# The first weights of each way up loaded on another queue, and three tiles in turn for one FFN factor

## The chip, the cores and the metric

One Trainium2 chip, one core. The metric is the device time of one execution in microseconds (us), as the median of timed runs. The engines are PE (matrix engine), VectorE (DVE), ScalarE (ACT), GpSimd (POOL) and SyncE (SP, which here only issues transfers). Each takes its own instructions strictly in order; they meet at semaphores. ScalarE, GpSimd and SyncE can issue transfers.

## The reference

Two transformer blocks over one sequence of 1024 rows of width 1024, in float32. What the change touches are the feed-forward parts; the mixers are left out here.

```python
def first_block(x, c, w_ada, ...):
    ...                                     # norm, three mixers, w_out, residual
    h = rms_norm(x, g_pre_ffn[l]) * (1.0 + sc_f) + sh_f
    up = dwconv3(h @ w_up[l], conv_w[l], conv_b[l])   # w_up: 1024 x 5632
    gate, val = jnp.split(up, 2, axis=-1)
    y = (jax.nn.gelu(gate) * val) @ w_down[l]         # 2816 x 1024
    x = x + gt_f * rms_norm(y, g_post_ffn[l])

def dwconv3(h, w, b):   # over positions, width 3, zero padded
    hp = jnp.pad(h, ((0, 0), (1, 1), (0, 0)))
    return hp[:, :-2] * w[0] + hp[:, 1:-1] * w[1] + hp[:, 2:] * w[2] + b

def _swiglu(x, w1, w3, w2):
    return (jax.nn.silu(x @ w1) * (x @ w3)) @ w2      # 1024 -> 2816 -> 1024

def second_block(x, ...):
    x = _layernorm(DEEPNORM_ALPHA * x + 0.5 * _swiglu(x, ffn1_w1[l], ffn1_w3[l], ffn1_w2[l]), ...)
    ...                                     # sparse attention and gated MLP, w_out
    x = _layernorm(DEEPNORM_ALPHA * x + 0.5 * _swiglu(x, ffn2_w1[l], ffn2_w3[l], ffn2_w2[l]), ...)
```

## The kernel before

The kernel goes through five large stages: the first block's mixer, the first block's FFN (`ffn1`), the second block's first FFN (`swiglu`), its mixer, and its second FFN (`swiglu` again). In the text T1 is the stretch in which `ffn1` begins, T2 that in which the first `swiglu` begins, T3 that in which the second one begins.

Every FFN has a way up and a way down. The way up is `up()`. It makes 22 output tiles f (128 hidden columns of each of the two factors, over 1024 positions), each out of seven products P = 1 to 7 of Strassen's scheme in Winograd's form, in the order 1, 2, 6, 7, 4, 5, 3. One product is 12 matmuls of 128 x 512: four slices of depth, each in three terms (`mm3`, lines 111 to 113), since every float32 operand is split into a high and a low half. Of the weights, ScalarE makes the high half `wh` (line 87) and VectorE or POOL the low half `wl` (line 106); POOL does it for products 1 and 5. POOL also makes the sums `T` of weight blocks that the products 4, 6, 7 need (line 264). Of the activations, `cross_xt()` transposes the normalised rows on PE (line 223) and makes the sums and halves `s23h`, `s23l`, `s4h`, `s4l` with POOL (lines 228, 231, 237), VectorE and ScalarE.

The weights of two tiles f come in one load of 1 MB for each factor: `load_cols` (line 125), 128 x 8 x 256 into a buffer `raw`. All of these loads are issued by POOL: with an engine given, `load_cols` pins the load into POOL's program order (`keep_in_program_order`), behind everything that the program wrote ahead of it for POOL. The first two loads of a way up (f = 0) are written at the start of `up()`, after the work of the stage before. In T1 the work ahead of them on POOL is the loop of `right()`, which prepares sums of the down weights in DRAM (`td`; lines 423, 432, 434). In T2 it is the additions of line 1724, which belong to the way down of `ffn1`.

Behind each f the products are added together (line 92, mostly VectorE) into the tiles 0 and 1 of `acc`, a buffer of eight tiles of 128 x 1024. In `ffn1` the function `glue` then makes both factors: `conv` is one ScalarE activation (line 1670) and two VectorE steps (line 101), g goes through gelu on ScalarE (line 1683), v is convolved likewise, and g becomes g·v (line 92, 128 x 1024). g lies in tile 2 and v in tile 3 of `acc` for even f, in 4 and 5 for odd f. `left()` then takes the two g tiles of a pair of f, makes their Winograd sums and stores them to `gd` in DRAM (`put`, line 389, on SP). The g tile of the even f is called e there: it takes up two of the sums (e + g and g − e), and the store of these is the last thing that reads it.

The order of instructions on each engine comes from a scheduler that goes by priorities and readiness, except for what is pinned. SP's own loads and stores are not pinned.

Of the kernel before, what the change touches and what calls it, by code (L numbers as in the profile page):

```python
# [20 lines left out]
FF = 2816  # L21
# [17 lines left out]
class Kern:  # L39
# [544 lines left out]
    def swiglu(self, w1, w3, w2, h1, ln, last, base, init, scale=None, bias=None, spill=None, during=None):  # L584


        tc, nc, acc = self.tc, self.nc, self.acc
        gd = self.dram.tile([NF // 2, 128, 7, 512], F32, name="gd" + ln[0])
        td = self.dram.tile([NF // 2, 128, 2, 1024], F32, name="td" + ln[0])

        def glue(f, P=None, done=None, c=None):
            g, v = acc[:, f % 2, :], acc[:, 2, :]
            if P is None:
                return g, v, g
            if P in (2, 4):
                nc.scalar.activation(out=g[:, c], in_=g[:, c], func=AF.Silu)
            if P != 2 and done >= ({2, 3} if P == 3 else {4, 5}):
                self.tt(g[:, c], g[:, c], v[:, c], OP.mult)

        self.stemps = self.unit_rows((3, 4))[:3]  # L600
        with tc.tile_pool(name="up", bufs=1, reuse_waits="tile") as pool:
            self.up(pool, [lambda f, w=w: self.load_cols(w, f * 128, eng=nc.gpsimd) for w in (w1, w3)], h1, glue,
                    scale, bias, gd, during, below=(w2, td))
        with tc.tile_pool(name="dn", bufs=1, reuse_waits="tile") as pool:
            for t in range(8):
                nc.gpsimd.dma_start(out=acc[:, t, :], in_=base[t * 128:(t + 1) * 128, :])
            tail = self.ln_tail(pool, ln, 4.0 * LN_EPS, last)
            self.down(pool, gd, td, w2, h1, tail, init, lambda: self.t4(pool, 5))
            if spill is not None:
                for t in range(8):  # L610
                    nc.gpsimd.dma_start(out=spill[t * 128:(t + 1) * 128, :], in_=acc[:, t, :])
# [1038 lines left out]
    def ffn1(self):  # L1650
        tc, nc, A = self.tc, self.nc, self.A
        xh, xl, acc = self.xh, self.xl, self.acc
        wu = A["w_up"][0]
        gd = self.dram.tile([NF // 2, 128, 7, 512], F32, name="gd")
        self.x2r = self.dram.tile([S, D], F32, name="x2r")
        self.stemps = self.unit_rows((6, 7))
        with tc.tile_pool(name="up", bufs=1, reuse_waits="tile") as pool:
            rows = [self.part(i, [88, 128]) for i in range(2)]
            for i in range(4):
                src = A["conv_w"][0, i] if i < 3 else A["conv_b"][0]  # L1660
                nc.scalar.dma_start(out=rows[i // 2][(i % 2) * 44:(i % 2) * 44 + 44, :],
                                    in_=src.rearrange("(r p) -> r p", p=128))
            ps = self.bankB([128, 2, 88])
            for i in range(2):
                nc.tensor.transpose(ps[:, i, :], rows[i], self.ident[:88, :88])
            cw = []

            def conv(u, h, j):

                nc.scalar.activation(out=u, in_=h, func=AF.Identity, scale=cw[0][:, 44 + j:45 + j],  # L1670
                                     bias=cw[0][:, 132 + j:133 + j])
                self.stt(u[:, 1:], h[:, :-1], cw[0][:, j:j + 1], u[:, 1:], OP.mult, OP.add)
                self.stt(u[:, :-1], h[:, 1:], cw[0][:, 88 + j:89 + j], u[:, :-1], OP.mult, OP.add)

            def glue(f, P=None, done=None, c=None):
                o = 2 + f % 2 * 2
                g, v = acc[:, o, :], acc[:, o + 1, :]
                h = [acc[:, i, :] for i in range(2)]
                if P is None:
                    return *h, g  # L1680
                if P in (2, 4) and done >= {2, 4}:
                    conv(g, h[0], f)
                    nc.scalar.activation(out=g, in_=g, func=AF.Gelu_apprx_tanh)
                elif P == 3:
                    conv(v, h[1], NF + f)
                    self.tt(g, g, v, OP.mult)

            def start():
                cw.append(pool.tile([128, 176], F32, name="cw"))
                self.copy(cw[0], ps.rearrange("p a b -> p (a b)"))  # L1690

            self.up(pool, [lambda f, o=o: self.load_cols(wu, o + f * 128, eng=nc.gpsimd) for o in (0, FF)], 0, glue,
                    self.gs_f, self.sh_f, gd, start=start)
        with tc.tile_pool(name="dn", bufs=1, reuse_waits="tile") as pool:
            pair = []
            gt = pool.tile([128, 1024], F32, name="gt")
            nc.sync.dma_start(out=gt, in_=self.gf_row.to_broadcast([128, 1024]))

            def room4():
                return pool.tile([128, 1024], F32, name="uv", tag="uv", bufs=4)  # L1700

            def tail(n, t):
                x = self.t4(pool, 2)
                nc.sync.dma_start(out=x, in_=self.x1d[t * 128:(t + 1) * 128, :])
                pair.append((t, x))
                if n == 0:
                    self.ss, self.junk = pool.tile([128, 8], F32, name="rss"), room4()
                with tc.high_priority() if n > 5 else nullcontext():
                    normed(n, t)
                if n % 2 and n < 4:  # L1710
                    self.later.append((n + LAG, lambda: self.keep_xt(t // 2)))

            def normed(n, t):
                a = acc[:, t, :]
                self.sumsq(self.ss[:, n:n + 1], a, self.junk)
                if n % 2 == 0:
                    return
                ss = self.ss[:, n - 1:n + 1]
                self.ts(ss, ss, 1.0 / D, OP.mult, RMS_EPS, OP.add)
                r = self.rsqrt(pool, ss, 2, "r2")  # L1720
                for i, (u, x) in enumerate(pair[-2:]):
                    a = acc[:, u, :]
                    self.stt(a, a, r[:, i:i + 1], gt, OP.mult, OP.mult)
                    (nc.vector if n > 5 else nc.gpsimd).tensor_tensor(out=a, in0=a, in1=x, op=OP.add)
                    nc.sync.dma_start(out=self.x2r[u * 128:(u + 1) * 128, :], in_=a)

            self.down(pool, gd, self.td, A["w_down"][0], 0, tail, None, room4)
# [737 lines left out]
```

## Time and profile before

| what | value |
|---|---|
| timed runs, median of 3 | 3225.34 us (3224.27 to 3226.1) |
| profiled execution, its own time | 3220.59 us |
| span of its trace | 3218.8 us |
| busy share: PE, VectorE, ScalarE, POOL | 91%, 74%, 39%, 36% |

The page of the profile gives busy times over the whole span. The rows further down are from narrower views: a table of busy times by stretch, timelines of one engine (each row is an instruction or a run of like ones, with the idle time before it and what ended that in brackets), and the table of waits (engine, line and tile that waited, what it waited for, the total, how often, the longest). "<-DMA x<-y" means that a transfer from y to x was waited for.

### The profile page before, as it was taken

What the parts mean: (1) busy time and instruction counts of PE and PEld (TensorE: products, weight loads), DVE (VectorE), ACT (ScalarE), POOL (GpSimd) and SP (SyncE); (2) the same over time, 40 slices, a digit from 0 to 9 for tenths busy, and PEclk for the clock granted to TensorE, in tenths of its full rate; (3) what the DMA queues carried; (4) which work ended last, traced back from release to release, by engine and by line L of the source; (5) the groups of instructions that cost most, each with busy time, mean ns of one, the idle gap of its engine ahead of it and who ended that gap; (6) DMA issues with size and microseconds to landing.
All of it is one profiled execution on the core that took longest, in us unless ns stands there. A gap on an engine that the chain in (4) does not pass through costs nothing. (4 is left out here: it accounts for less than half of the span.)

```text
span 3218.8 us, 38064 instructions
## 1 busy us (share of the span) xinstructions
PE 2932.0 (91%) x13810; PEld 2317.2 (72%) x13810; DVE 2368.8 (74%) x3855; ACT 1249.0 (39%) x2023; POOL 1168.6 (36%) x1001
## 2 busy tenths in 40 slices
PE   6899996799898999699999999977999799999996
PEld 4675565677777887578887888875677677887885
DVE  6982656887878656877776577799857887777567
ACT  5122532433333443323222443557762422222442
POOL 4422267655544002645553001131313655453003
PEclk9899998899999999799999999989999899999998
DMA  6116364222222673344444773110012265444762
GB/s 212 55 34 246 136 199 156 72 87 84 93 85 91 233 229 133 118 161 151 152 159 168 253 246 105 41 34 1 14 68 104 78 237 190 156 160 167 264 213 88
DMA packets 175508, 440.18 MB, mean 137 GB/s; under 512 B 16296, under 2 KB 36040, under 8 KB 175192
## 3 DMA queue, kind: packets, MB, share of 16 engines
q1 hardware_dynamic: 138924, 307.20, 27.4%
q0 software_dynamic: 36032, 130.19, 12.3%
q8 instruction: 109, 1.79, 0.2%
q14 instruction: 79, 0.65, 0.1%
q10 hardware_dynamic: 364, 0.35, 0.0%
HBM read 315.41 MB, written 122.27 MB: 136 GB/s over the span
## 5 line engine op out<-in xcount | busy, mean ns | idle before, releaser
L87 ACT ACTIVATE wh<-raw 128x512 fp32r<-128x512 f32 (+1 forms) x506 | 407.3, 826 | 839.6 <-PE bB L112 207.9
L106 DVE TENSOR_TENSOR wl<-raw,wh 128x1024 fp32r<-128x1024 f32 (+1 forms) x370 | 439.3, 1193 | 245.0 <-ACT wh L87 243.6
L111 PE MATMUL bB<-xh,wh 128*128 128x512 f32 (+1 forms) x860 | 343.3, 399 | 4.7 <-ACT xh L87 4.5
L112 PE MATMUL bB<-xl,wh 128*128 128x512 f32 (+1 forms) x860 | 340.3, 396 | 4.2 <-DVE xl L106 4.2
L113 PE MATMUL bB<-xh,wl 128*128 128x512 f32 (+1 forms) x860 | 339.5, 395 | 0.7 <-DVE wl L106 0.6
L92 DVE TENSOR_TENSOR acc<-acc 128x512 f32<-128x512 f32 (+2 forms) x306 | 306.7, 1015 | 19.6 <-DMA gdln_g<-acc 9.5
L106 POOL TENSOR_TENSOR wl<-raw,wh 128x512 fp32r<-128x512 f32 (+1 forms) x136 | 220.7, 1625 | 220.1 <-ACT wh L87 210.3
L111 PE MATMUL bA<-xh,wh 128*128 128x512 f32 (+1 forms) x508 | 211.4, 417 | 90.0 <-DVE acc L92 53.3
L264 POOL TENSOR_TENSOR T<-raw 128x512 f32<-128x512 f32 x132 | 200.1, 1516 | 182.9 <-DMA raw<-in_ffn_w 96.4
L92 DVE TENSOR_TENSOR acc<-bA,acc 128x512 f32<-128x512 f32 x226 | 150.4, 685 | 127.4 <-PE bA L113 127.1
L92 DVE TENSOR_TENSOR acc<-bB,acc 128x512 f32<-128x512 f32 x260 | 178.1, 686 | 69.2 <-PE bB L113 58.7
L264 POOL TENSOR_TENSOR T<-raw,T 128x512 f32<-128x512 f32 x66 | 106.8, 1619 | 309.4 <-DVE wl L106 307.0
L112 PE MATMUL bA<-xl,wh 128*128 128x512 f32 (+1 forms) x508 | 208.2, 411 | 1.0 <-DVE xl L106 1.0
L113 PE MATMUL bA<-xh,wl 128*128 128x512 f32 (+1 forms) x508 | 207.8, 409 | 0.2 <-DVE wl L106 0.2
L111 PEld LDWEIGHTS bB<-xh,wh 128*128 128x128 f32 x860 | 164.0, 191 | 46.8 <-ACT xh L87 6.0
L112 PEld LDWEIGHTS bB<-xl,wh 128*128 128x128 f32 x860 | 163.6, 190 | 44.6 <-DVE xl L106 5.9
L87 ACT ACTIVATE wh<-T 128x512 fp32r<-128x512 f32 x198 | 118.2, 624 | 191.9 <-PE bA L112 88.9
L113 PEld LDWEIGHTS bB<-xh,wl 128*128 128x128 f32 x860 | 163.4, 190 | 39.5 <-DVE wl L106 1.3
L111 PEld LDWEIGHTS bA<-xh,wh 128*128 128x128 f32 x508 | 101.5, 200 | 122.6 <-ACT wh L87 73.2
L101 DVE SCALAR_TENSOR_TENSOR acc<-acc,cw 128x1023 f32<-128x1023 f32 x88 | 138.6, 1576 | 62.2 <-ACT acc L1670 61.7
L111 PE MATMUL bA<-wh 128*128 128x512 f32 x432 | 170.5, 395 | 12.8 <-DVE acc L92 12.8
L112 PE MATMUL bA<-wl,wh 128*128 128x512 f32 x432 | 169.7, 393 | 0.0
(527 smaller groups left out, 7401.9 us busy)
## 6 DMA issues: line engine op xcount, KB each, us to landing
raw<-in_ffn_w POOLq DMA_DIRECT2D x44, 1024.0 KB, 6.1
raw<-gdln_g SPq DMA_DIRECT2D x70, 512.0 KB, 4.1
raw<-in_w_up POOLq DMA_DIRECT2D x22, 1024.0 KB, 6.2
tq<-in_ffn_w SPq DMA_DIRECT2D x44, 512.0 KB, 4.9
tdln_g<-tq SPq DMA_DIRECT2D x44, 512.0 KB, 2.6
gdln_g<-acc SPq DMA_DIRECT2D x44, 512.0 KB, 2.6
raw<-tdln_g SPq DMA_DIRECT2D x40, 512.0 KB, 5.0
raw<-gd SPq DMA_DIRECT2D x35, 512.0 KB, 4.0
```

The lines of the kernel that those rows point to most:

```text
L87: self.nc.scalar.activation(out=out, in_=in_, func=AF.Copy)
L92: self.nc.vector.tensor_tensor(out=out, in0=a, in1=b, op=op)
L101: self.nc.vector.scalar_tensor_tensor(out=out, in0=a, scalar=s, in1=b, op0=op0, op1=op1)
L106: (eng or self.nc.vector).tensor_tensor(out=lo, in0=src, in1=hi.bitcast(F32), op=OP.subtract)
L111: mm(out, lhsT=wh, rhs=xh, start=start, stop=False)
L112: mm(out, lhsT=wh, rhs=xl, start=False, stop=False)
L113: mm(out, lhsT=wl, rhs=xh, start=False, stop=stop)
L264: sub = lambda o, a, b: nc.gpsimd.tensor_tensor(out=o, in0=a, in1=b, op=OP.subtract)
```

## The change

Two edits. First, in both ways up the two loads of f = 0 are issued without an engine given, so they go to SP's queue and aren't pinned; the loads of all later f stay on POOL. Second, in `ffn1` the tile of g is 2, 3 or 4 by f modulo 3, and v always has tile 5.

```diff
@@ swiglu
-            self.up(pool, [lambda f, w=w: self.load_cols(w, f * 128, eng=nc.gpsimd) for w in (w1, w3)], h1, glue,
+            self.up(pool, [lambda f, w=w: self.load_cols(w, f * 128, eng=f and nc.gpsimd) for w in (w1, w3)], h1, glue,
                     scale, bias, gd, during, below=(w2, td))
@@ ffn1, glue
-                o = 2 + f % 2 * 2
-                g, v = acc[:, o, :], acc[:, o + 1, :]
+                g, v = acc[:, 2 + f % 3, :], acc[:, 5, :]
                 h = [acc[:, i, :] for i in range(2)]
@@ ffn1
-            self.up(pool, [lambda f, o=o: self.load_cols(wu, o + f * 128, eng=nc.gpsimd) for o in (0, FF)], 0, glue,
+            self.up(pool, [lambda f, o=o: self.load_cols(wu, o + f * 128, eng=f and nc.gpsimd) for o in (0, FF)], 0, glue,
                     self.gs_f, self.sh_f, gd, start=start)
```

How this moves instructions, at three places. SP's queue between the last loads of the first mixer (`in_w_out`) and the stores of its result rows (`x1d`), as the difference:

```order
 L1596 DMA raw<-in_w_out 128x1024 x3
 L1600 DMA raw<-in_w_out 64x1024 x4
+L125 DMA raw<-in_w_up 128x8x256 x2
 L1642 DMA x1d<-t_3070 128x1024
 L1642 DMA x1d<-t_3157 128x1024
```

The two first loads of the first FFN now stand ahead of all the stores of the mixer's result. POOL at the same transition, where `tq` and `td` belong to the loop of `right()`:

```order
 L432 TENSOR_TENSOR tq<-tq 128x256 x4
 L434 DMA td<-tq 128x2x256 x2
-L125 DMA raw<-in_w_up 128x8x256 x2
 L106 TENSOR_TENSOR wl<-raw,wh 128x512 x2
 L228 TENSOR_TENSOR raw<-acc 128x256 x2
```

POOL's rows around them keep their order; only the loads are gone. POOL in T2, with the additions of the way down (`acc` plus a residual row tile `t_...`), before:

```order
L1724 TENSOR_TENSOR acc<-acc,t_8418 128x1024
L1724 TENSOR_TENSOR acc<-acc,t_8597 128x1024
L1724 TENSOR_TENSOR acc<-acc,t_8625 128x1024
L125 DMA raw<-in_ffn_w_2 128x8x256 x2
L106 TENSOR_TENSOR wl<-raw,wh 128x512 x2
L228 TENSOR_TENSOR raw<-acc 128x256 x2
```

and of the changed kernel, where the same addition has line 1723:

```order
L1723 TENSOR_TENSOR acc<-acc,t_8418 128x1024
L106 TENSOR_TENSOR wl<-raw,wh 128x512 x2
L1723 TENSOR_TENSOR acc<-acc,t_8597 128x1024
L1723 TENSOR_TENSOR acc<-acc,t_8625 128x1024
L228 TENSOR_TENSOR raw<-acc 128x256 x2
L231 TENSOR_TENSOR acc<-acc 128x2x128
```

The low halves of the first product now stand ahead of two additions of the stage before. On ScalarE the four `wh<-raw` moved in the same way, from behind the last four L836 rows to ahead of the last `acc<-bB` rows and of these; on SP the two loads stand ahead of the last four stores `x2r`; on PE seven matmuls of the first product stand between two groups of the way down, and a second group of 16 transposes (line 223) has gone behind the first-half products. In T3 only the loads moved, from POOL to SP's queue ahead of its stores `x2n`. In the way up of `ffn1` a few rows of f = 2 and 3 changed places on ScalarE, VectorE and PE; from f = 4 on the order is as before.

## Rows read from the trace of the kernel before

**Rows 1.** Table by stretch: bounds, us, busy us (instructions), granted PE clock, DMA share, GB/s.

```profile
700.00:1000.00 300.00, 275.00 (x1121) 219.17 (x1121) 235.41 (x253) 104.57 (x146) 147.65 (x95) 0.95 0.27 92
1286.00:1373.00 87.00, 57.40 (x247) 45.91 (x246) 71.68 (x94) 31.85 (x64) 60.86 (x53) 0.76 0.36 121
1400.00:1700.00 300.00, 300.00 (x1288) 241.50 (x1287) 223.18 (x278) 87.69 (x152) 152.30 (x109) 1.00 0.45 156
2505.00:2574.00 69.00, 47.87 (x231) 39.52 (x229) 65.05 (x92) 30.57 (x57) 47.02 (x41) 0.83 0.25 85
```

**Rows 2.** Timelines, T1, ScalarE and PE: start, us, instruction, count [idle before <-releaser].

```profile
541.92 0.63 ACT L87 ACTIVATE wh<-raw 128x512 fp32r<-128x512 f32 x1 [22.60 <-DMA raw<-in_w_up]
...
543.64 0.80 PE L111 MATMUL bA<-xh,wh 128*128 128x512 f32 x1 [26.52 <-ACT wh L87]
```

**Rows 3.** Timeline of POOL, T1.

```profile
535.72 1.80 POOL L125 DMA_DIRECT2D raw<-in_w_up  x2
542.64 2.95 POOL L106 TENSOR_TENSOR wl<-raw,wh 128x512 fp32r<-128x512 f32 x2 [5.11 <-ACT wh L87]
547.74 1.91 POOL L228 TENSOR_TENSOR raw<-acc 128x256 f32<-128x256 f32 x2 [2.15 <-DVE acc L98]
```

**Rows 4.** Timeline of SP's queue, ahead of T1.

```profile
414.82 2.39 SPq L1600 DMA_DIRECT2D raw<-in_w_out  x4
445.81 0.33 SPq L1642 DMA_DIRECT2D x1d<-t  x1
```

**Rows 5.** Waits of 610 to 1040 us: who, for what, us in total, times, longest.

```profile
DVE acc L101 <- ACT acc L1670: 57.8, 33, 4.0
...
ACT acc L1670 <- DMA gd<-acc: 41.7, 8, 6.6
...
PE bA L111 <- DVE acc L92: 37.3, 11, 4.6
```

**Rows 6.** Timelines of one pair of f in the first FFN's way up.

```profile
815.65 1.25 ACT L1670 ACTIVATE acc<-acc,cw 128x1024 f32<-128x1024 f32 x1 [4.88 <-DMA gd<-acc]
...
825.12 1.25 ACT L1670 ACTIVATE acc<-acc,cw 128x1024 f32<-128x1024 f32 x1 [0.86 <-DVE acc L92]
...
795.85 0.69 DVE L92 TENSOR_TENSOR acc<-bA,acc 128x512 f32<-128x512 f32 x1 [0.92 <-PE bA L113]
...
806.12 1.22 DVE L92 TENSOR_TENSOR acc<-acc 128x1024 f32<-128x1024 f32 x1
...
812.65 0.69 DVE L92 TENSOR_TENSOR acc<-bB,acc 128x512 f32<-128x512 f32 x1 [0.47 <-PE bB L113]
816.93 2.25 DVE L101 SCALAR_TENSOR_TENSOR acc<-acc,cw 128x1023 f32<-128x1023 f32 x1 [3.59 <-ACT acc L1670]
...
826.40 1.29 DVE L101 SCALAR_TENSOR_TENSOR acc<-acc,cw 128x1023 f32<-128x1023 f32 x1 [1.31 <-ACT acc L1670]
...
791.24 0.47 PE L111 MATMUL bA<-xh,wh 128*128 128x512 f32 x1 [2.80 <-DVE acc L92]
836.76 0.77 PE L111 MATMUL bA<-xh,wh 128*128 128x512 f32 x1 [4.55 <-DVE acc L92]
```

**Rows 7.** Timelines of POOL, ScalarE, VectorE and PE, T2.

```profile
1286.25 1.78 POOL L125 DMA_DIRECT2D raw<-in_ffn_w  x2
...
1295.30 2.19 ACT L87 ACTIVATE wh<-raw 128x512 fp32r<-128x512 f32 x4 [6.61 <-DMA raw<-in_ffn_w]
...
1296.48 3.05 DVE L106 TENSOR_TENSOR wl<-raw,wh 128x512 fp32r<-128x512 f32 x2 [6.40 <-ACT wh L87]
...
1296.50 0.80 PE L111 MATMUL bA<-xh,wh 128*128 128x512 f32 x1 [8.04 <-ACT wh L87]
...
1372.66 0.80 PE L111 MATMUL bA<-xh,wh 128*128 128x512 f32 x1 [7.37 <-DVE acc L92]
```

**Rows 8.** Timelines of ScalarE and PE, T3.

```profile
2500.41 2.19 ACT L87 ACTIVATE wh<-raw 128x512 fp32r<-128x512 f32 x4 [13.27 <-PE bA L113]
...
2573.74 0.64 PE L111 MATMUL bA<-xh,wh 128*128 128x512 f32 x1 [4.34 <-DVE acc L92]
```

## The prediction, made before the changed kernel ran

> **What bounds the kernel now.** I read the table by stage first [rows 1]. The engine to follow is the matrix engine, PE. In the way up of the third stage (1400 to 1700 us) it is busy 300.00 of 300 us at granted clock 1.00, with 1288 matmuls: 0.233 us each, so 168 (two output tiles f, a pair) take 39.1 us, and nothing can be gained there. In the first FFN's way up (700 to 1000 us) the same matrix work runs at 1121 matmuls in 300 us, 45.0 us a pair, with PE busy 275.00 at clock 0.95: something holds PE there once in a while. At the entry of the third stage (1286 to 1373) PE is busy 57.40 of 87 us at 0.76. The entry of the last FFN (2505 to 2574), which does nearly the same work, needs 69 us. So I read three places: the entry of the first FFN (T1), its way up, and the entry of the third stage (T2). The last FFN's entry (T3) is the comparison. For each place I went to the timelines and looked at the idle time in front of PE and what ended it, then followed that engine back, until I stood at a wait for a transfer.
>
> **T1, the first loads on SP's queue.** PE stands still for 26.52 us until 543.64, released by ScalarE's first rounding of weights (wh). ScalarE had waited 22.60 us for the transfer raw<-in_w_up [rows 2]. That transfer was issued by POOL at 535.72, at once after work of its own (no idle is shown), and landed in time for 541.92, 6.2 us later [rows 3]. SP had finished its w_out loads at about 417 and its next row is at 445.81 [rows 4]. The changed order puts the loads into that hole, so they land more than 90 us before anyone can use them. ScalarE could then start at 541.92 − 22.60 = 519.3. What is late next is POOL: the low half wl of the first product is POOL's own, behind the same row of work that ends at 535.72. It started at 542.64; without the load it starts at 535.72, 6.92 us earlier. POOL's next idle, 2.15 us before 547.74, waits for VectorE's chain, which starts with wh and so is early too [rows 3]. 6.92 + 2.15 = 9.1. The two issues themselves (1.80 us on POOL) are inside this sum. Against it: 2 MB now move around 417 to 428, beside the loads of POOL's own loop. If that loop, which sets 535.72, is pushed by the whole landing time of 6.2, less than 3 us is left. The other end is the whole 22.6, if POOL's wl didn't bind. I take −8, near POOL's row, because POOL shows no idle there; −3 to −13 goes into the range.
>
> The Trainium skill ("DMA: Bandwidth & Descriptors", section "Issuing engines are not separate DMA queues") speaks against expecting much: transfers of all issuing engines run on the same 16 DMA engines, and issuing from another one saves only issue time on the sequencer. By it, T1 and T2 would give 1.80 + 1.78 us. The row of ScalarE's 22.60 us disagrees, as that is the wait for a late issue and not for slow bytes.
>
> **The way up of the first FFN, three tiles for g.** In the waits of 610 to 1040 us, ScalarE's convolution of g (L1670) waits 8 times for DMA gd<-acc, 41.7 us in all; VectorE's second step (L101) waits for ScalarE's conv 57.8 us in 33 waits; PE waits for VectorE 37.3 us in 11 [rows 5]. One pair shows how they hang together [rows 6]. At 815.65 the conv of an even f starts, 4.88 us late, because its g tile still holds the pair's e sum, which is being stored. VectorE stands 3.59 us before 816.93. At 826.40, where the tile is free, the same wait is 1.31, ScalarE's own time. VectorE is in order, so everything behind L101 comes 3.59 − 1.31 = 2.28 later: the sums that free PE's banks among it, and PE's gap of 4.55 before 836.76 is the end of it. Check from the other side: VectorE's addition that feeds the conv ends at 812.65 + 0.69 = 813.34, and 813.34 + 1.31 = 814.65, which is 2.28 before 816.93. With three tiles in turn the e tile of a pair is g again three f later, not two, and its stores have a whole f more to land: the wait is gone. 8 × 2.28 = 18.2 us. PE's gaps (2.80 and 4.55 in the rows) are larger than 2.28, so PE takes all of it. The order on ScalarE and VectorE stays as it was from f = 4 on.
>
> On top, a shorter gap may leave PE less at half clock: VectorE waits 0.92 and 0.47 us for PE's slow products behind a gap (795.85 and 812.65) [rows 6]. That is 0 to 1.39 a pair, 0 to 11 us. The rows show clock 0.95 with these gaps and 1.00 with none [rows 1], and gaps of some 2 us remain, so I take a third: −4. Together −22.
>
> The second factor v has one tile now. The product g·v frees it at 806.12 + 1.22 = 807.34; the next conv of v starts at 825.12 [rows 6]. 17.8 us hide this edit, which I cost at nothing.
>
> **T2.** POOL issues the loads at 1286.25, behind its additions of the stage before; ScalarE waits 6.61 for them until 1295.30, PE 8.04 until 1296.50, VectorE 6.40 until 1296.48, and then makes its wl for 3.05 before it returns to the normalisation chain that PE waits for next [rows 7]. In the changed order SP loads before the last stores x2r, ScalarE rounds before its last four L836 rows, wl on both engines is made during the way down, and seven of the first matmuls stand between the last two kept tiles. The low bound is the PE gap less an added delay of 3: −5. One chain gives −8.04 to −(6.40 + 3.05) = −9.5. The high bound is T3, whose loads were always early and whose order T2 now nearly has: from PE's last work of the stage before to the first matmul behind the entry, T2 takes 1372.66 − 1286 = 86.7 [rows 7] and T3 2573.74 − 2505 = 68.7 [rows 8], −18. I take −12: past the chain, since more than one gap closes in T3, but not all, since T3 has fewer matmul rows in its window (231 against 247 [rows 1]). The edit adds a wait: ScalarE's four roundings now stand ahead of two groups of rows from PE's banks and the L836 rows, and POOL's two wl ahead of two additions; if their slots aren't free, all of these wait.
>
> **T3.** The load moves too, but nothing waited for it: ScalarE's wh at 2500.41 waits 13.27 us for PE [rows 8]. 0.
>
> **The sum.** −8 − 22 − 12 = −42 against the profiled execution of 3220.6 (span 3218.8), 3178.6. The median of the timed runs is 4.7 above the profiled one, so 3225.3 − 42 = 3183. Own range of this case: T1 −3 to −13, way up −18 to −26, T2 −5 to −18; not all ends together: 3172 to 3194.
>
> **Rivals.**
> 1. All of it pays: the clock's 11 us whole and T2 like T3. −8 − 29 − 18 = −55, 3170. For it: gaps end where VectorE ends. Against: gaps remain. 0.15.
> 2. The wait in the way up only moves: VectorE is busy 235.41 of 300 us [rows 1] and gets to another wait (for POOL's sums or for the store behind the product), so that some 5 of 22 us are left. −25, 3200. For it: all engines of a pair are chained, and the store's landing time sets one more wait. Against: the product and its store move forward together. 0.11.
> 3. The loads give only their issue time: no more than 1.80 + 1.78 = 3.6 on POOL, because the buffers or SP's order hold them until late, or another producer was late with them. −22 − 4 = −26, 3200. The rule of the Trainium skill on issuing engines, named above, would give this time too. Against: SP's hole at 417 to 445 [rows 4]. 0.05.
> 4. T2's roundings wait for their slots, as in T3: 13.27 us [rows 8] in front of ScalarE's last normalisations, and PE's kept tiles wait. T2 is then +1 and not −12. −8 − 22 + 1 = −29, 3196. Against: in T3 the same wait stood beside PE work. 0.08.
> 5. Slower: the single v tile. If the conv of v comes to wait for the product of the f before, which decides once the 17.8 us of slack are used up by the moved order, each of 22 f pays about what a g tile cost a pair, 2.28: +50 and no gain in the way up. −8 − 12 + 50 = +30, 3255. Against: the slack is eight times the price. 0.04.
> 6. The gains of T1 and the way up are given back by collisions and less than 6.5 us is left: 3222. 0.04.
>
> **How the numbers follow.** The forecast has 0.53, the rivals 0.15, 0.11, 0.05, 0.08, 0.04, 0.04. Cases 1 to 4 and the forecast are all faster by over 0.2% (6.5 us, about what a measurement of this kernel can tell from no change): 0.92. Within 0.2%: 0.04, slower 0.04. The range that should hold 8 in 10 takes the forecast's own range, rival 1 in part and rivals 2 to 4: 3166 to 3203.
>
> **What would show it.** Right: in the waits of the changed way up no line "ACT acc L1670 <- DMA gd<-acc" of any size, VectorE's L101 waits near 1.3, PE's gaps near 1.3 to 2.3, and a pair in 42 to 43 us. In T1 no wait for raw<-in_w_up on ScalarE before some 520, POOL's wl at about 536 without idle before it, PE's first pause ended by wl near 537. In T2 no wait for raw<-in_ffn_w, and about 75 us to the point that was 86.7. Wrong: a wait of POOL or ScalarE in the way down before T2, a conv of v that waits for VectorE's product, or a pair that still takes 45 us with another releaser in front of L101; and T1's POOL loop ending later than 535.7.

## The result, and the profile after

The changed kernel takes 3175.73 us (median of 4 runs, 3172.97 to 3180.37); the kernel before, beside it, 3224.81 (4 runs). The ratio is 0.9855, 95% interval 0.9833 to 0.9877: 49 us faster by the medians, where 42 were forecast. The two profiled executions have spans of 3218.8 and 3174.7 us, 44.1 apart.

Where it went is read best from five marks that every run has: A, the start of the last matmul of the first mixer's output (line 1634); B, the matmul of the first FFN's way up that follows PE's gap of about 3.2 us for VectorE (bA<-s23h, at 612.02 in the trace of before; in l231_vec the gap in front of it is 0.9 us); C, the start of the last convolution step (L1670); D, the last addition of POOL in the way down (L1724); E, the last issue of the loads acc<-x2r in the way down of the second block's first FFN. Table of the stretches in us, all from profiled runs:

| run | A | A to B (T1) | B to C (way up) | C to D (way down) | D to E (T2 and what follows) | E to end |
|---|---|---|---|---|---|---|
| before | 516.7 | 95.3 | 453.4 | 218.5 | 498.4 | 1436.5 |
| after | 518.8 | 89.4 | 419.1 | 217.5 | 492.4 | 1437.5 |
| glue_only | 520.8 | 93.3 | 421.6 | 217.4 | 498.8 | 1437.2 |
| loads_only | 519.3 | 85.2 | 455.3 | 217.5 | 493.1 | 1433.9 |
| pool_unpinned | 532.9 | 93.3 | 420.8 | 222.5 | 494.0 | 1439.5 |
| late_td | 519.2 | 72.2 | 432.4 | 217.6 | 493.5 | 1435.4 |
| late_td2 | 518.9 | 72.6 | 424.8 | 217.4 | 493.4 | 1436.9 |
| late_td4 | 520.3 | 70.9 | 437.2 | 217.5 | 492.9 | 1436.9 |
| delay2 | 519.3 | 85.0 | 428.5 | 217.3 | 493.1 | 1436.7 |
| delay3 | 518.9 | 84.1 | 426.3 | 217.4 | 493.6 | 1436.6 |
| conv2 | 521.6 | 85.2 | 423.8 | 218.4 | 493.4 | 1437.5 |
| conv3 | 523.2 | 85.4 | 432.2 | 218.7 | 491.7 | 1435.9 |
| t2_no_add | 518.2 | 89.4 | 419.1 | 217.5 | 491.2 | 1437.0 |
| l231_vec | 523.0 | 83.1 | 419.5 | 217.5 | 489.6 | 1437.2 |

Between before and after: T1 −5.9, way up −34.3, way down −1.0, T2 −6.0, the rest +1.0, and +2.1 that lie ahead of A, where the computing is the same (glue_only, without the moved loads, has A later still). That is −44.1. A stretch that two kernels share can differ by more than 5 us from trace to trace: A goes from 516.7 to 523.2, without pool_unpinned, and the way from E to the end from 1433.9 to 1439.5. D to E is steadier: 491.7 to 493.6 in the changed kernel and the eight others with the same T2.

The table by stretch of the changed kernel (columns as in [rows 1]): the way up of the first FFN, T2, and the last FFN's entry T3.

```profile
700.00:1000.00 300.00, 292.09 (x1246) 233.15 (x1244) 262.97 (x283) 117.68 (x163) 164.55 (x102) 1.00 0.28 98
...
1246.00:1325.00 79.00, 49.36 (x230) 40.87 (x229) 67.48 (x92) 30.48 (x61) 52.31 (x46) 0.77 0.32 110
...
2459.00:2528.00 69.00, 47.71 (x230) 39.31 (x227) 64.78 (x92) 30.59 (x57) 46.60 (x41) 0.83 0.26 84
```

Against [rows 1], the way up has 1246 matmuls in the 300 us that held 1121, and the granted clock is 1.00 and no longer 0.95. T3 hasn't moved. T2 is shorter than its 87 us, but with as many matmuls as T3 it still takes 10 us more.

**T1**, timelines of PE and POOL in the changed kernel, which answer to [rows 2, 3]; and the first loads of POOL's loop in the kernel before and in the changed one, to give that loop a start:

```profile
520.42 0.50 PE L111 MATMUL bA<-xh,wh 128*128 128x512 f32 x1 [1.21 <-ACT wh L87]
542.50 0.80 PE L113 MATMUL bB<-xh,wl 128*128 128x512 f32 x1 [16.88 <-POOL wl L106]
...
541.17 2.49 POOL L106 TENSOR_TENSOR wl<-raw,wh 128x512 fp32r<-128x512 f32 x2
543.62 1.41 POOL L228 TENSOR_TENSOR raw<-acc 128x256 f32<-128x256 f32 x2
...
420.05 2.89 POOL L423 DMA_DIRECT2D tq<-in_w_down  x4
```

```profile
417.26 2.89 POOL L423 DMA_DIRECT2D tq<-in_w_down  x4
```

PE's first matmul of the FFN no longer waits for a load. Its long wait came back a few matmuls later, for POOL's wl, which has no idle ahead of it. POOL's loop took 541.17 − 420.05 = 121.1 us; before it was 535.72 [rows 3] − 417.26 = 118.5.

**The way up**, waits of 600 to 1025 us, which answer to [rows 5]; then timelines of PE and VectorE, which answer to [rows 6]:

```profile
DVE acc L101 <- ACT acc L1670: 39.9, 36, 1.3
...
PE bA L111 <- DVE acc L92: 15.5, 10, 3.8
...
DVE acc L92 <- DMA gd<-acc: 2.5, 8, 0.3
```

```profile
737.35 0.47 PE L111 MATMUL bA<-xh,wh 128*128 128x512 f32 x1 [1.48 <-DVE acc L92]
777.82 0.47 PE L111 MATMUL bA<-xh,wh 128*128 128x512 f32 x1 [1.04 <-ACT wh L87]
818.19 0.47 PE L111 MATMUL bA<-xh,wh 128*128 128x512 f32 x1 [0.93 <-DVE acc L92]
...
820.15 2.16 DVE L101 SCALAR_TENSOR_TENSOR acc<-acc,cw 128x1023 f32<-128x1023 f32 x1 [0.55 <-ACT acc L1670]
...
828.17 2.60 DVE L101 SCALAR_TENSOR_TENSOR acc<-acc,cw 128x1023 f32<-128x1023 f32 x2 [1.31 <-ACT acc L1670]
```

The longest wait of L101 is 1.3 us, where it was 4.0. No wait of ScalarE's convolution for gd<-acc is left among the larger ones, and VectorE's small one (2.5 us) is no new one: it was 2.6 before. In these rows one pair of f takes 40.4 to 40.5 us and PE's gaps are 0.9 to 1.5 us; over the whole way up, from 690 us on, they are 0.7 to 1.7.

**T2**, timelines of ScalarE, POOL and PE, which answer to [rows 7]:

```profile
1217.39 2.20 ACT L87 ACTIVATE wh<-raw 128x512 fp32r<-128x512 f32 x4 [2.12 <-DMA raw<-in_ffn_w]
...
1244.82 2.39 POOL L1723 TENSOR_TENSOR acc<-acc,t 128x1024 f32<-128x1024 f32 x1 [1.16 <-DVE acc L101]
1251.16 1.87 POOL L228 TENSOR_TENSOR raw<-acc 128x256 f32<-128x256 f32 x2 [3.95 <-DVE rs_y L98]
...
1264.67 2.24 POOL L264 TENSOR_TENSOR T<-raw 128x512 f32<-128x512 f32 x1
...
1251.14 0.50 PE L111 MATMUL bB<-xh,wh 128*128 128x512 f32 x1 [0.87 <-DVE acc L199]
1267.63 0.58 PE L111 MATMUL bA<-s23h,wh 128*128 128x256 f32 x1 [7.59 <-ACT wh L87]
1272.80 0.58 PE L112 MATMUL bA<-s23l,wh 128*128 128x256 f32 x1 [4.58 <-DVE s23l L106]
...
1323.45 0.77 PE L111 MATMUL bA<-xh,wh 128*128 128x512 f32 x1 [4.80 <-DVE acc L92]
```

The roundings end some 20 us ahead of PE's first use of them, and PE's 8.04 us [rows 7] have become 0.87. A gap of 7.59 us stands 16 us further on, where the kernel before has 4.92, and behind it one of 4.58. The 7.59 us are a wait for the high half of a sum T, which POOL makes only behind its whole chain of cross sums. For the start of that chain and the first T in the kernel before, rows of its POOL that weren't shown, and PE's gap there:

```profile
1283.91 2.40 POOL L1724 TENSOR_TENSOR acc<-acc,t 128x1024 f32<-128x1024 f32 x1 [1.16 <-DVE acc L101]
...
1300.01 1.86 POOL L228 TENSOR_TENSOR raw<-acc 128x256 f32<-128x256 f32 x2 [1.03 <-DVE rs_y L101]
...
1308.77 2.25 POOL L264 TENSOR_TENSOR T<-raw 128x512 f32<-128x512 f32 x1
...
1315.08 0.58 PE L111 MATMUL bB<-s23h,wh 128*128 128x256 f32 x1 [4.92 <-ACT wh L87]
```

From POOL's last addition to the first T it is 24.9 us before (1308.77 − 1283.91) and 19.9 after (1264.67 − 1244.82), so T comes 5.0 us earlier. The chain itself begins 9.8 us earlier. The difference is the order: before, seven rows of the chain stood ahead of the first T and five behind the T sums; now all twelve stand ahead of it.

The matmul at 1323.45 answers to the one at 1372.66 [rows 7]. From D it comes 10.1 us earlier (78.63 us, before 88.75), but 17 matmuls (4.0 us) that stood ahead of it in the kernel before now stand behind it. Like for like that is again 6.

### The profile page after: what moved, and what is told of

It is laid out like the page before. It is cut to its first block, busy times and chain, and to the rows that moved or that the text cites. A ratio compares the mean times of both kernels' runs of the same rounds, so it can differ in the third digit from the quotient of the medians.

```text
span 3174.7 us, 38064 instructions
## 1 busy us (share of the span) xinstructions
PE 2915.9 (92%) x13810; PEld 2304.4 (73%) x13810; DVE 2367.9 (75%) x3855; ACT 1250.5 (39%) x2023; POOL 1156.5 (36%) x995
## 5 line engine op out<-in xcount | busy, mean ns | idle before, releaser
L92 DVE TENSOR_TENSOR acc<-acc 128x512 f32<-128x512 f32 (+2 forms) x306 | 314.3, 1039 | 36.7 <-POOL raw L228 17.8
L92 DVE TENSOR_TENSOR acc<-bA,acc 128x512 f32<-128x512 f32 x226 | 150.2, 684 | 123.7 <-PE bA L113 123.2
L111 PE MATMUL bA<-xh,wh 128*128 128x512 f32 (+1 forms) x508 | 204.8, 404 | 35.3 <-DVE acc L92 29.4
L101 DVE SCALAR_TENSOR_TENSOR acc<-acc,cw 128x1023 f32<-128x1023 f32 x88 | 139.3, 1583 | 41.7 <-ACT acc L1670 41.2
L113 PE MATMUL bA<-wh,wl 128*128 128x512 f32 x432 | 169.9, 393 | 0.0
```

The source lines that it names most:

```text
L92: self.nc.vector.tensor_tensor(out=out, in0=a, in1=b, op=op)
L101: self.nc.vector.scalar_tensor_tensor(out=out, in0=a, scalar=s, in1=b, op0=op0, op1=op1)
L111: mm(out, lhsT=wh, rhs=xh, start=start, stop=False)
L113: mm(out, lhsT=wl, rhs=xh, start=False, stop=stop)
```

## The experiments

**The two edits apart.** glue_only takes back the first edit (in both ways up), loads_only the second.

```diff
-eng=f and nc.gpsimd
+eng=nc.gpsimd
...
-g, v = acc[:, 2 + f % 3, :], acc[:, 5, :]
+o = 2 + f % 2 * 2
+g, v = acc[:, o, :], acc[:, o + 1, :]
```

> Only the three g tiles and the single v tile; all first loads stay on POOL as before. Theory (the way up of the first FFN loses VectorE's 2.28 us a pair and, since PE then stays at the full clock, also what VectorE waited for PE's slow products; the changed kernel showed 34 us between the first and the last convolution): 34 us faster than before, about 3190, a pair in 40.6 us, T1 and T2 as before (ScalarE waits 22 us and 6 to 7 us for the loads). Rival (part of those 34 us came from the earlier start and the moved rows of f = 2 and 3, the tile itself gives the forecast 22): 3203.

> Only the first loads on SP's queue; g and v tiles in pairs as before. Theory (T1 is left bound by POOL's td loop, T2 by VectorE and POOL): T1 6 us, T2 6 us, together 12 us faster than before, about 3213; the pairs of the way up still take 45.2 us. Rival (issuing from another queue saves only the issue time on POOL): 3.6 us, 3221. Rival (the two entries only gain because the way up behind them no longer stalls): no change.

Measured: glue_only 3187.77 us, 0.9892 of before (0.9878 to 0.9907), 34.2 us by the medians (the kernel before, beside it, 3221.98); way up −31.8, T2 +0.4. loads_only 3207.17 us, 0.9958 (0.9943 to 0.9972), 14.8 us; T1 −10.1, T2 −5.3, way up +1.9. The two add up to 49, which is the whole. So the tiles are worth some 34 and the loads some 15, and neither needs the other. In glue_only the theory of 34 us holds, and in loads_only that of 12. The 3.6 us that the loads should save by the rule of the Trainium skill ("DMA: Bandwidth & Descriptors", section "Issuing engines are not separate DMA queues"), an estimate from the issue times 1.80 + 1.78, lie outside loads_only's interval.

**Is it the queue or the place in the order?** pool_unpinned leaves the first loads on POOL without pinning them (both ways up pass `eng=nc.gpsimd, pin=f`).

```diff
-        if eng:
+        if eng and pin:
             self.tc.keep_in_program_order(i)
```

> As the changed kernel, but the first loads are issued by POOL again, without being pinned into its program order: they now stand near the front of POOL's td loop in T1 instead of behind it, and in T2 ahead of the additions of the way down. Theory (what pays is the place in an engine's order, not the queue): the same as the changed kernel within 5 us, 3171 to 3181, ScalarE without a wait of over 3 us for raw<-in_w_up. Rival (SP's queue itself pays): near 3190, as with the tiles alone.

Measured: 3183.32 us, 0.9892 (0.9857 to 0.9927). Its profiled run is the slowest of its four (3204.81 us, the others 3177.89 to 3184.25) and was 14 us late ahead of mark A, so only the stretches behind it count, and they come from an odd execution. Timelines of its PE, POOL and ScalarE:

```profile
559.39 0.80 PE L113 MATMUL bB<-xh,wl 128*128 128x512 f32 x1 [15.99 <-POOL wl L106]
...
434.37 2.90 POOL L423 DMA_DIRECT2D tq<-in_w_down  x4
...
558.06 2.50 POOL L106 TENSOR_TENSOR wl<-raw,wh 128x512 fp32r<-128x512 f32 x2
...
1232.77 2.10 ACT L87 ACTIVATE wh<-raw 128x1024 fp32r<-128x1024 f32 x3 [6.16 <-DMA raw<-in_w_down]
```

The early load took ScalarE's wait away here too, yet T1 is only 2.0 us shorter than before. POOL's loop, with two issues in it, takes 558.06 − 434.37 = 123.7 us, and that loop is what T1 now hangs on. In T2 the stretch D to E gains 4.4 us, but the way down loses 4.0, with a wait of 6.16 us for its own weights. My theory said that only the place counts. It holds for the wait. In this one trace it doesn't hold for the time: the place on POOL's own queue costs about what it saves. The medians don't settle that, as 3183.32 lies between the 3171 to 3181 of the theory and the 3190 of the rival, and the interval touches that of the changed kernel.

**What T1 hangs on now.** late_td moves the last of the eight rounds of POOL's td loop into the way up, late_td2 moves it in two halves (256 columns each, loaded at f = 6 and 10), late_td4 in four quarters (128 columns, f = 4, 8, 12, 16); each computes one f later. The functions below are the first mixer's output, and in `ffn1` one that is called at the first product of each f, as late_td has it.

```diff
+                if t < 7:
                     self.right(pool, A["w_down"][0], self.td, 3 + t, 256, 2)()
...
+            def late(f):
+                if f == 6:
+                    td_sums.append(self.right(pool, A["w_down"][0], self.td, 10, 256, 1))
+                elif f == 7:
+                    td_sums.pop()()
```

> As the changed kernel, but the last of the eight rounds of POOL's td loop ahead of T1 is moved into the way up of the first FFN (f = 6 and 7). Theory (in T1 PE now waits 16.9 us for POOL's wl, which stands behind that loop): POOL is at wl 12 to 15 us earlier, PE's wait shrinks to 2 to 5 us, and the kernel is 8 to 14 us faster than the changed one, 3162 to 3168; in the way up one or two pairs may be up to 2 us longer. Rival (VectorE's chain or the transposes bind T1 next, or the round costs as much in the way up): within 4 us of the changed kernel.

> As late_td, but the moved round of POOL's td loop is cut into two halves that stand four output tiles apart (f = 6, 7 and f = 10, 11). In late_td the entry T1 got 17 us shorter than in the changed kernel, but two gaps of PE (4.3 and 6.0 us) and what followed them in the pair with the second half took most of it back. Theory (a half round fits into POOL's idle time of a pair, two in a row don't): the changed kernel less 12 to 16 us, 3160 to 3164. Rival (each half stalls the pair's chain anyway): 3170 to 3176.

> As late_td2 with the moved round in quarters (f = 4, 8, 12, 16 load, the f behind each computes). The halves took T1's 17 us and gave back 5.6 in the way up, where two pairs were 2 to 3 us longer. Theory (a quarter fits into POOL's idle time): the way up as in the changed kernel, 2 to 5 us faster than late_td2, 3160 to 3168. Rival (more instructions and smaller rows eat it): the same as late_td2 or slower.

Measured: late_td 3171.69 us (0.9842, 0.9826 to 0.9859), late_td2 3170.42 (0.9842, 0.9827 to 0.9857), late_td4 3173.18 (0.9837, 0.9804 to 0.987). Timelines of late_td: PE and POOL in T1, then PE and POOL around the moved round.

```profile
522.02 0.50 PE L111 MATMUL bA<-xh,wh 128*128 128x512 f32 x1 [2.45 <-ACT wh L87]
...
523.12 2.51 POOL L106 TENSOR_TENSOR wl<-raw,wh 128x512 fp32r<-128x512 f32 x2
...
741.52 0.64 PE L111 MATMUL bB<-xh,wh 128*128 128x512 f32 x1 [4.27 <-DVE acc L92]
752.13 0.80 PE L111 MATMUL bA<-xh,wh 128*128 128x512 f32 x1 [6.04 <-DVE acc L92]
...
732.45 1.31 POOL L264 TENSOR_TENSOR T<-raw,T 128x512 f32<-128x512 f32 x1
```

T1 went from 89.4 to 72.2 us, so the theory of T1 is right: POOL's loop was the bound, 17 us of it. The way up paid for it: 432.4 against 419.1, since the sum T at 732.45 came late behind the moved round. The halves pay 5.7 there and the quarters 18.1, so the theory that smaller pieces fit better fell: in late_td4 every second pair has a gap of 4.2 us. Late_td2 is 11 us shorter than the changed kernel in the trace, which is its fastest run, and 5 us in the medians. The times of all three miss the theories (8 to 14 and 12 to 16 us faster than the changed kernel, and 2 to 5 us faster than late_td2) and lie about where the rivals put them.

**Is a pair dearer than VectorE's delay?** Four kernels put a delay back into 8 pairs of the changed one: delay2 and delay3 as idle multiplications on VectorE, conv2 and conv3 by repeating ScalarE's convolution step. The diff has delay2 first and then conv2; delay3 and conv3 have a 3 for the 2.

```diff
+                    if f in range(4, 19, 2):
+                        for _ in range(2):
+                            self.tt(v, v, v, OP.mult)
                     conv(g, h[0], f)
...
+                for _ in range(2 if j in range(4, 19, 2) else 1):
                     nc.scalar.activation(out=u, in_=h, func=AF.Identity, ...)
```

> As the changed kernel, with two idle multiplications of 128x1024 (1.2 us each) on VectorE ahead of the convolution of g in 8 even f (4 to 18), about the 2.28 us a pair that the change took from VectorE. They write the tile of v, which is overwritten afterwards, so all results stay. Theory (the gain of a pair is larger than VectorE's wait, since a short gap costs PE its full clock): the pairs go back from 40.6 to about 44 to 45 us and the granted clock of the way up from 1.00 to 0.95 to 0.97, 26 to 36 us slower than the changed kernel. Rival (a pair pays just what VectorE is held): 8 x 2.4 = 19 us slower with the clock near 1.00. Rival (VectorE has slack now): under 8 us.

> As delay2 with three multiplications. Theory (the clock already fell with two, so the third costs its own length in each pair or a little more): 8 x 1.2 = 10 to 14 us slower than delay2. Rival (each one costs the same from the first on): half as much again as delay2 over the changed kernel.

> As the changed kernel, with ScalarE's first step of the convolution of g made twice (the second writes the same values) in 8 even f, 4 to 18. VectorE's L101 behind it, and ScalarE's queue, are held 1.2 us longer in each of these pairs; before the change it was 2.28 us longer for VectorE. (The idle multiplications of delay2 and delay3 went into VectorE's idle time and held nobody.) Theory (a delay in this chain opens PE's gap, and beyond some 2 us of gap PE also loses its full clock): the gap is 1.0 + 1.2 = 2.2, just at the edge, so 8 x 1.2 = 10 to 18 us slower than the changed kernel. Rival (VectorE and ScalarE have slack since the change): under 5 us.

> As conv2 with three instead of two, some 2.3 us or more of delay a pair, as much as the change took away. Theory: the pairs return to about 45 us, PE's gaps to 3 to 4.5 us with a first matmul of 0.77 instead of 0.47 us behind them, granted clock 0.95 to 0.96; 30 to 38 us slower than the changed kernel. Rival (PE pays only VectorE's delay): 18 us, clock near 1.00. Rival (it was ScalarE's late wh for the next products, which stand behind the waiting convolution, and not VectorE): also about 18 to 38, but then PE's gaps end with ScalarE's wh or VectorE's wl and not with VectorE's sums.

Measured: delay2 3181.48 us (0.988, 0.9864 to 0.9897), delay3 3178.75 (one run), conv2 3176.95 (0.9851, 0.9822 to 0.9881), conv3 3188.06 (0.9886, 0.9856 to 0.9916); in the way up +9.4, +7.2, +4.7 and +13.1 us over the changed kernel. The wait of delay3; the stretch, two gaps and the 10 us behind each in conv3; and the 10 us behind the gap of 2.80 [rows 6] in the kernel before:

```profile
DVE acc L101 <- ACT acc L1670: 15.1, 16, 1.3
```

```profile
700.00:1000.00 300.00, 284.63 (x1200) 227.15 (x1201) 260.08 (x272) 128.34 (x169) 170.24 (x102) 0.99 0.28 97
...
742.57 0.47 PE L111 MATMUL bA<-xh,wh 128*128 128x512 f32 x1 [2.68 <-DVE acc L92]
785.72 0.47 PE L111 MATMUL bA<-xh,wh 128*128 128x512 f32 x1 [2.17 <-DVE acc L92]
...
743.00:753.00 10.00, 10.00 (x38) 7.95 (x37) 7.37 (x8) 4.49 (x6) 6.81 (x5) 0.83 0.35 119
786.00:796.00 10.00, 10.00 (x44) 8.06 (x43) 7.97 (x9) 5.08 (x6) 8.26 (x6) 1.00 0.37 126
```

```profile
792.00:802.00 10.00, 10.00 (x38) 7.94 (x37) 7.04 (x8) 4.69 (x6) 6.48 (x5) 0.83 0.33 108
```

The multiplications are no test of the question. The three (8 x 3.6 = 29 us of work) fell for the most part into VectorE's waits for ScalarE, which shrank from 39.9 to 15.1 us, and the clock of the way up stayed at 1.00 in both kernels. In conv3 VectorE has other work in the longer wait: L101 still waits 1.3 us at most. PE's gaps came back to 1.9 to 2.7 us and no further, with the clock at 0.99. The two rows of 10 us have 0.83 and 1.00. So behind the gap of 2.68 us part of the work ran at the lower level (1.2 GHz, half of the full 2.4), though the first matmul there is short. Of conv3's eight gaps two were followed by that, those of 2.68 and 2.07 us, and six of 1.9 to 2.2 us were not. In the kernel before, all eight gaps (2.8 to 4.65 us) were, with 0.80 to 0.91 in the 10 us behind each; in the changed kernel none of eight was.

The expectations fell. Delay2 and conv3 are some 6 and 12 us slower than the changed kernel by the medians, where 26 to 36 and 30 to 38 were expected. Delay3, a single run, isn't slower than delay2, where 10 to 14 were expected. Conv2 is 1.2 us slower, where 10 to 18 were, so its rival (under 5) holds. None of them rebuilds the old state. That a delay of 2.28 us alone brings back the 34 is therefore not shown. Late_td4, with gaps of 4.2 us in every second pair, has clock 0.98:

```profile
768.59 0.76 PE L111 MATMUL bA<-xh,wh 128*128 128x512 f32 x1 [4.20 <-DVE acc L92]
...
810.91 0.47 PE L111 MATMUL bA<-xh,wh 128*128 128x512 f32 x1 [0.70 <-DVE acc L92]
...
700.00:1000.00 300.00, 284.62 (x1192) 227.00 (x1191) 259.90 (x270) 112.46 (x156) 172.72 (x123) 0.98 0.29 99
```

**What T2 hangs on.** t2_no_add leaves out VectorE's residual additions of the last two tiles, l231_vec gives POOL's sum of line 231 to VectorE in all entries (diffs in this order).

```diff
-    (nc.vector if n > 5 else nc.gpsimd).tensor_tensor(out=a, in0=a, in1=x, op=OP.add)
+    if n < 6:
+        nc.gpsimd.tensor_tensor(out=a, in0=a, in1=x, op=OP.add)
...
-    nc.gpsimd.tensor_tensor(out=hf[:, 0], in0=hf[:, 0], in1=hf[:, 1], op=OP.add)
+    self.tt(hf[:, 0], hf[:, 0], hf[:, 1], OP.add)
```

> As the changed kernel, but the residual additions of the last two rows of tiles in the first FFN's way down are left out, which VectorE makes within T2 (3.94 us for the two); this part of the result is missing. Theory (T2 is now bound by VectorE's own work, of which T3 has less): T2 is 3 to 5 us shorter, 3171 to 3173. Rival (POOL's chain of sums binds T2): within 1.5 us of the changed kernel.

> As the changed kernel, but the sum that ScalarE's xh waits for in each entry (line 231) is made by VectorE instead of POOL, 8 per entry. Leaving VectorE's 3.9 us of additions out of T2 gained only 1.2 us there, so VectorE alone doesn't bind T2. Theory (POOL's chain of sums, which stood without a pause for 13.5 us ahead of the T sums, binds T2): T2 gets 3 to 6 us shorter, the kernel 3167 to 3172 or a little less with the other entries. Rival (VectorE, busy 85% of T2 and 94% of T3, binds): 2 to 8 us slower.

Measured: t2_no_add 3173.02 us (0.985, 0.9835 to 0.9865), D to E 1.2 us shorter than in the changed kernel. l231_vec 3171.76 us (0.983, 0.9797 to 0.9863), D to E 2.8 shorter. Rows of PE in T2, of t2_no_add and of l231_vec:

```profile
1267.79 0.58 PE L112 MATMUL bA<-s23l,wh 128*128 128x256 f32 x1 [0.72 <-DVE s23l L106]
...
1322.06 0.77 PE L111 MATMUL bA<-xh,wh 128*128 128x512 f32 x1 [6.75 <-DVE acc L92]
```

```profile
1261.90 0.38 PE L111 MATMUL bA<-s23h,wh 128*128 128x256 f32 x1 [3.64 <-ACT wh L87]
...
1322.57 0.79 PE L111 MATMUL bA<-xh,wh 128*128 128x512 f32 x1 [8.08 <-DVE acc L92]
```

Without the additions the gap of 4.58 us in front of s23l is 0.72, but the last gap of the entry is 6.75 and was 4.80. With the sum on VectorE the gap of 7.59 is 3.64, and the last one 8.08. Each time the end of T2 takes most of it back. In l231_vec the first T comes 15.9 us behind POOL's last addition, 4.0 earlier than in the changed kernel, for 2.8 us of T2. Neither VectorE's additions nor this part of POOL's chain binds T2 alone. The 1.2 us can't be told from none, since D to E differs by 1.9 us among kernels with the same T2; the 2.8 stand out of that, and are less than the 3 to 6 us that I expected, though the time of l231_vec lies inside its 3167 to 3172. In t2_no_add the rival (within 1.5 us) holds for T2.

**A version that beats both?** late_td, late_td2 and l231_vec have medians 4 to 5 us below the changed kernel's, but all these intervals overlap with 0.9833 to 0.9877. They beat the kernel before; that they beat the changed one isn't shown.

## Why the prediction was right, and which terms were off

The time lies inside the range and the direction is the forecast one. The sum of −42 against −44.1 in the traces holds two errors that offset each other: the way up gave 12 us more than forecast and T2 6 less. That the total came so close is luck.

**T1, −8: right.** The trace of the changed kernel has −5.9, loads_only −10.1, and the four delay kernels, with the same T1, −9.9 to −11.2. The step that made the number is confirmed: POOL's wl starts at the end of its td loop, with no idle before it. But one sign of being wrong came: the loop ends at 541.17, and not by 535.7. Of these 5.5 us 2.8 lie ahead of the loop (its first load is at 420.05 and was at 417.26), and 2.7 in it. The 2.7 are most of what the 5.9 lack to the 9.1 of POOL's row. That the two loads beside the loop lengthen it isn't shown, for what varies is the loop itself: 121.1 us in the changed kernel and 121.3 in t2_no_add, 117.6 to 119.0 in the delay kernels (first load of the loop to wl), for one and the same order. Late_td shows it from the other side, with one round less and 17 us. The prediction named 22.6 as the end if POOL didn't bind, and that is where late_td and late_td2 go.

**The way up, −22: right in its mechanism as far as the rows go, too small by 12.** The −34.3 lie outside the range of −18 to −26, and beyond the −29 of rival 1. The first term is met: VectorE's waits for ScalarE's convolution went from 57.8 [rows 5] to 39.9, −17.9 for the forecast 18.2. The mis-sized term is the clock, "−4 of 0 to 11". What it measured is in two rows, per pair of 168 matmuls. Idle of PE: 25.00/1121 x 168 = 3.75 us before, 7.91/1246 x 168 = 1.07 after, −2.7. PE's busy time: 275.00/1121 x 168 = 41.2 us before, 292.09/1246 x 168 = 39.4 after, −1.8. Over 8 pairs that is 21 and 15, together 36; the marks show 34.3. So the clock paid 15 and not 4, and the gaps 21 and not 18.2. The step failed in two places. I bounded the clock's price by what VectorE waited for PE (0.92 and 0.47 a pair), but PE's slow matmuls cost PE itself their whole extra length, whoever waits. And I let gaps of some 2 us remain at a slow clock. They are 0.7 to 1.7, with the clock at 1.00, and even conv3's gaps of 1.9 to 2.7 leave it at 0.99. The row that would have given it was in [rows 1]: 0.95 of the clock over 41 us of work is 2 us a pair. The single v tile costs nothing that any of these runs shows: the moves of rows of f = 2 and 3 and that tile are in glue_only, which has the whole gain. That VectorE's wait opened PE's gaps is read from the rows and not shown by an experiment, since none of the four delays brought the gaps back in full.

**T2, −12: half of it.** It measured −6.0 (−5.3 in loads_only). The chain's part of it was met: PE's 8.04 and VectorE's 6.40 are gone, and POOL's first cross sum follows the last addition after 6.3 us (1251.16 − 1244.82), where it was 16.1 (1300.01 − 1283.91), so 9.8 earlier. The step that failed is the one beyond the chain, the comparison with T3. T3's 69 us aren't T2's end: with 230 matmuls in both, T2 still takes 79. Even the sign that I named, about 75 us to the point that was 86.7, nearly came, at 10.1 less; but 4.0 of that is work which the changed order puts behind this point. Inside T2 some 4 us of the 9.8 were given back. The rows show where: the changed order puts the first T behind POOL's whole chain, so it comes only 5.0 us earlier. The two experiments moved 1.2 (no clear change) and 2.8 of T2; which of the other chains holds the rest is open.

**The rivals.** Rival 1 (all of it pays) was right for the way up and wrong for T2. Rival 2 (the wait in the way up only moves) is out by the waits and by glue_only, rival 3 (issue time alone) by loads_only. Rival 4 (T2's roundings wait for slots) is out: ScalarE's wait there is 2.12 us and for the load, and the way down ahead of T2 is no longer for it (−1.0). Rival 5 (the v tile) didn't come: in the stretch of 690 to 790 us the product g·v ends some 12 us ahead of the next convolution of v, where it was 17.8. Rival 6 didn't come either.

## What to carry to other kernels

A load that stands behind an engine's own work in that engine's order is late by that work, and the gain of moving it ends at the next thing on the same engine: look at what else sits behind the same loop before counting the whole wait. When the matrix engine's work has gaps, read the granted clock of that stretch against one without gaps, and not the length of the first matmul behind a gap; the slower matmuls are a price of their own, beside the gap. When one stage is measured by another that looks alike, count what each engine still has to do in it, and do not take the shorter one as the end.

## What the runs showed of the hardware

- The granted clock of the first FFN's way up went from 0.95 to 1.00 when PE's gaps, one a pair, shrank from 2.8 to 4.65 us down to 0.7 to 1.7 us. With gaps of 1.9 to 2.7 us (conv3) it was 0.99, with 4.2 us in every second pair (late_td4) 0.98.
- The first matmul behind a gap doesn't tell the clock: it took 0.47 us behind 2.80 us in the kernel before [rows 6] and behind 2.68 us in conv3, and in the 10 us behind either the granted clock was 0.83.
- POOL's loop of 64 subtractions with its transfers took 117.6 to 121.3 us in kernels whose order of instructions there is the same.
- Idle multiplications of 3.6 us a pair on VectorE cost 0.9 us a pair (7.2 us over 8 pairs, one trace), while its waits for ScalarE shrank by 24.8 us.
